# A decode step with paged attention: cache pages requested two page pairs ahead, and the first head of each superblock's attention requested some steps before its first logits

## The chip, the cores and the metric

The kernel runs on one core of a Trainium2 chip. The metric is the device time of one execution in microseconds, from the runs shown, with the median as the kernel's time. One further execution was recorded by the hardware profiler; all rows below come from it.

## The reference, cut to what matters

One layer of a hybrid decoder. A prompt of 2048 tokens (after 16 meta tokens) and 8 samples of 8 new tokens each go through one input projection whose columns are queries, keys, values, and the two inputs of a recurrent branch; then attention and recurrence side by side, an output projection, and a squared-ReLU MLP. The attention is stick-breaking: for each query a running product of "keep" factors goes over the keys from the last to the first.

```python
z = einsum('bqhd,bkhd->bhqk', q, k) * HEAD_DIM ** -0.5 + bias
log_keep = where(mask, log_sigmoid(-z), 0.0)
suffix = cumsum(log_keep, axis=3, reverse=True) - log_keep
w = where(mask, exp(log_sigmoid(z) + suffix), 0.0)
out = einsum('bhqk,bkhd->bqhd', w, v)
```

The samples attend to 512 past positions each, which lie in 4 pages of 128 rows in a key cache and a value cache; a page table says which pages (`cache_k[page_table]`, `cache_v[page_table]`). Everything is float32.

## The kernel before, in words

**The main line.** The prompt is cut into four superblocks of 512 tokens. For each, `inproj` (line 432) multiplies by the input projection: eight `gemm` calls for the recurrent branch (x and gate, alternating), four for keys, one `gemm_nat` of four weight tiles for values, four `gemm` calls for queries. Every float32 matmul is three matmuls of split operands (lines 181 to 183 and 213 to 215): a weight tile `wraw` is loaded on SP, split into `whi` by ACT (line 158) and `wlo` by DVE (line 159). After the four projections come, for each superblock, the output projection (`out_proj`), and the MLP (`up` and `down`, four slices each). The order of TensorE (PE) is written out by hand: it is the order in which the program emits its matmuls. The order on ACT, DVE, POOL and SP is not written by hand; it is set when the program is built, from the dependencies, the buffers that come free and the order of writing, so a load can stand on its queue ahead of instructions that were written before it.

**The side line.** Attention is written as generators that are woven into the main line by the class `Work` (line 37). Each `yield busy, pe` ends a step and states its cost in units; `tick(c)` (line 61), called after every few matmuls of the main line, adds `c * rate` to a debt, and steps are taken until the debt is used up. Three matmuls of 512 columns count 0.64 units of `c`; `gemm` ticks after k = 2, 5 and 7 (line 186, that is `c` of 1.92, 1.92 and 1.28), `gemm_nat` with 1.28 after each row block. The rate is 0.2 during the recurrent part of superblocks 1 to 3, 0.5 in their key, value and query part and in `up`, and 0.55 in `down` (line 1198). The second number of a yield is only added to `work.now`, which nothing reads. The order of the side line is fixed (lines 1101 to 1103): first `sample_attn`, then `attn(0)` to `attn(3)`, each from the time at which its keys and queries are written. `need(key)` (line 74) takes all the steps that are left of a generator at once, without main matmuls between them. `group(0)` (line 1117) calls it for `attn(0)` right after the first query `gemm` of the last superblock (lines 1131 to 1137); two more query `gemm` calls follow (`NQ` is 3), in which `Group.load` fetches the attention's result `md` for the first output projection, and then `out_proj`. The superblocks 1 to 3 are asked for in the same way before the last `down` slice of the superblock ahead.

**The samples' attention** (`sample_attn`, line 809) runs four rounds t_, two samples each. `weights(t_)` makes the logits of the new keys (line 825), then for four page pairs calls `page`, which takes a tile "kv" and issues two indirect DMAs on POOL's queue (line 817), and multiplies (line 840); a chain of sigmoids on ACT, a scan and a product on DVE (`chain`, line 629) makes the weights. `values(t_)` transposes them (lines 855 and 859), copies them to `wt` (tag "q", on ACT) and `wtn` (on DVE, line 861), multiplies the new values (line 869 with `vns`), then again calls `page` for four page pairs and multiplies each (line 869 with `kv`).

**The prompt's attention** (`attn(s)`, line 650) goes over 8 heads; a head has s + 1 groups of keys. `head(h)` (line 658) takes a tile "q" and loads the queries (line 661, 512 KB) and the top keys and values (lines 665 and 666); `kv_load(n)` (line 673) loads the keys and values of one group (lines 678 to 680 or 683 and 684). All go out on POOL's queue. In the generator `s_items` the first step calls `head(0)`, `head(1)`, `kv_load(0)`, `kv_load(1)` and then the first logits (line 694); transposes (line 705, `emit_T`) follow some steps later, are split into `wth` (ACT, line 709) and `wtl` (DVE, line 710), and `emit_V` multiplies (lines 720 and 721). After the last logits of a superblock 13 steps are left: three empty ones, then transposes and value products.

**Buffers.** The tag "kv" has three buffers, shared by the pages and by `kv_load`. The tag "q" has two, shared by `wt` and by the queries of `head`.

Of the kernel before, what the change touches and what calls it, by code (L numbers as in the profile page):

```python
# [84 lines left out]
def _program(tc, I, O, NSB, NSC):  # L85
# [18 lines left out]
    def T(p, shape, dt, tag, bufs=1):  # L104
        uid[0] += 1
        return p.tile(shape, dt, name=f"{tag}_{uid[0]}", tag=tag, bufs=bufs)
# [543 lines left out]
    def attn(s, K):  # L650
# [82 lines left out]
        def s_items():  # L733

            for n, (h, g) in enumerate(groups):
                H = head(h)
                if g == s:
                    head(h + 1) if live["kvt"] < 3 else None
                while live["kv"] > 2:
                    yield None  # L740
                kv_load(n)
                kv_load(n + 1)
                head(h)
                kvt = kvs.pop(n)
                if g == 0:
                    vt = {j: (kvt[:, 400 + P * j:528 + P * j], NMETA + P * j, P) for j in range(3)}
                    vt[-1] = (kvt[0:NMETA, 784:784 + P], 0, NMETA)
                else:
                    vt = {4 * g - 1 + j: (kvt[:, 512 + P * j:640 + P * j], P * j, P) for j in range(4)}
                wtop = None  # L750
                if g == s:
                    while live["w"] >= WB:
                        yield None
                    wtop = logits(H, h, 3, H["kt"][:, 0:P], P, 0)
                    yield 0.6
                ws = []
                for i in range(4):
                    nt = (min(i, 2) + 2) if g == s else 4
                    m = nt * P - (P - NMETA if g == 0 else 0)
                    kap = kvt[:, 0:m]  # L760
                    mask = m - P if (g == s and i < 3) else None
                    while live["w"] >= WB:
                        yield None
                    ws.append(logits(H, h, i, kap, m, mask))
                    if i < 3:
                        yield 1.25 * m / 512
                tl = []
                if g == s:
                    for j in range(3):
                        vap, c0, kn = vt[4 * s + j]  # L770
                        tl.append((vap, kn, j, [(i, ws[i], c0) for i in range(j, 4)]))
                    tl.append((H["kt"][:, P:2 * P], P, 3, [(3, wtop, 0)]))
                    vap, c0, kn = vt[4 * s - 1]
                    tl.append((vap, kn, 0, [(i, ws[i], c0) for i in range(4)]))
                else:
                    for t_ in sorted(vt, reverse=True):
                        vap, c0, kn = vt[t_]
                        tl.append((vap, kn, 0, [(i, ws[i], c0) for i in range(4)]))
                for ti, (vap, kn, i0, parts) in enumerate(tl):
                    e = ti == len(tl) - 1  # L780
                    top = g == s and ti == 3
                    tq.append(dict(at=step[0] + 4, v=vap, kn=kn, i0=i0, parts=parts, H=H, h=h,
                                   first=(g == s and ti == 0), last=(g == 0 and e), endg=e, top=top,
                                   frees=(4 if e else 0) + (1 if top else 0)))
                yield 1.25 * m / 512

        src = s_items()
        more = True
        while more or tq or vq:
# [19 lines left out]
    def sample_attn(K, p1):  # L809
        ck = I["cache_k"]  # L810
        cv = I["cache_v"]

        def page(src, b, pp):
            t = T(att, [P, 2, 512], F32, "kv", 3)
            for e in range(2):
                j = b * NPAGE + 2 * pp + e
                nc.gpsimd.indirect_dma_start(out=t[:, e, :], out_offset=None, in_=src,
                                             in_offset=bass.IndirectOffsetOnAxis(ap=K["ix"][:, j:j + 1], axis=0))
            return t

        def weights(t_):
            sn = psT()
            for c in range(4):
                for bb in range(2):
                    nc.tensor.matmul(sn[32 * c:32 * c + 32, 0:NSAMP], K["Qz"][:, c, t_, bb, :], K["kns"][:, c, :],
                                     start=(bb == 0), stop=(bb == 1))
            zn = T(att, [P, NSAMP], F32, "zn", 1)
            nc.vector.tensor_tensor(zn, sn[:, 0:NSAMP], K["maskS"][:, t_, :], op=ALU.add)
            wn, carry = chain(zn, NSAMP, K["brow"], K["nbrow"], None)
            yield 0.7, 1.0  # L830
            sp = psT()
            nc.tensor.matmul(sp, K["zb"][:, 0:P], K["zb"], start=True, stop=False)
            for bb in range(2):
                for pp in range(2):
                    kp = page(ck, 2 * t_ + bb, pp)
                    yield 0.3, 0.0
                    for e in range(2):
                        g = 2 * pp + e
                        for c in range(4):
                            nc.tensor.matmul(sp[32 * c:32 * c + 32, g * P:(g + 1) * P], K["Qz"][:, c, t_, bb, :],  # L840
                                             kp[:, e, c * P:(c + 1) * P], start=False, stop=False)
                        yield 0.3, 0.3
            nc.tensor.matmul(sp, K["zb"][:, 0:P], K["zb"], start=False, stop=True)
            w, _ = chain(sp, 512, K["brow"], K["nbrow"], carry)
            out[t_] = (w, wn)
            yield 1.8, 0.0

        out = {}
        smix = T(p1, [P, 4, NSAMP], F32, "smix")

        def values(t_):
            w, wn = out[t_]
            tp = psT()
            for pg in range(4):
                nc.tensor.transpose(tp[:, pg * P:(pg + 1) * P], w[:, pg * P:(pg + 1) * P], ident)
            wt = T(att, [P, 4, P], F32, "q", 2)
            nc.scalar.copy(wt.rearrange("p a b -> p (a b)"), tp)
            tp = psT()
            nc.tensor.transpose(tp[0:NSAMP, 0:P], wn[:, 0:NSAMP], ident)
            wtn = T(att, [NSAMP, P], F32, "wtn", 1)  # L860
            nc.vector.tensor_copy(wtn, tp[0:NSAMP, 0:P])
            yield 1.0, 0.6
            yield 1.0, 0.0
            o = psO()

            nc.tensor.matmul(o[:, 0:2 * P], K["zb"][:, 0:P], K["zb"][:, 0:2 * P], start=True, stop=False)

            def av(c, bb, w, v):
                nc.tensor.matmul(o[32 * c:32 * c + 32, bb * P:(bb + 1) * P], w, v, start=False, stop=False)

            for c in range(4):
                for bb in range(2):
                    av(c, bb, wtn[:, 32 * c:32 * c + 32], K["vns"][:, c * P:(c + 1) * P])
            for bb in range(2):
                b = 2 * t_ + bb
                for pp in range(2):
                    vp = page(cv, b, pp)
                    yield 0.3, 0.0
                    for e in range(2):
                        for c in range(4):  # L880
                            av(c, bb, wt[:, 2 * pp + e, 32 * c:32 * c + 32], vp[:, e, c * P:(c + 1) * P])
                        yield 0.3, 0.3
            nc.tensor.matmul(o[:, 0:2 * P], K["zb"][:, 0:P], K["zb"][:, 0:2 * P], start=False, stop=True)
            ot = T(att, [P, 512], F32, "beta", WB)
            nc.scalar.copy(ot[:, 0:2 * P], o[:, 0:2 * P])
            yield 0.5, 0.0
            yield 0.5, 0.0
            tp = psT()
            for bb in range(2):
                nc.tensor.transpose(tp[:, bb * P:(bb + 1) * P], ot[:, bb * P:(bb + 1) * P], ident)  # L890
            ov = tp[:, 0:2 * P].rearrange("p (x c b h q) -> p x c b h q", x=2, c=4, b=2, h=2)
            for hh in range(2):
                r = slice(64 * hh, 64 * hh + 64)
                for bb in range(2):
                    b = 2 * t_ + bb
                    nc.scalar.copy(smix[r, :, b * DS:(b + 1) * DS], ov[r, bb, :, bb, hh, :])
            yield 0.5, 0.2

        for t_ in range(4):
            yield from weights(t_)  # L900
            yield 1.0, 0.0
            yield from values(t_)
        nc.sync.dma_start(msd[:, 0:4, :], smix)
        yield 1.0, 0.0
# [376 lines left out]
```

## Time and profile before

| | us |
|---|---|
| median of 3 runs | 2818.16 (2817.05 to 2828.23) |
| the profiled execution, its own time | 2818.91 |
| its span, first to last instruction | 2817.1 |
| PE busy | 2719.1 (97%) |
| DVE, ACT, POOL busy | 1787.8, 1450.0, 692.4 |
| samples' attention on PE | from 184 to 434 |
| attention of superblock 0 on PE | from 438 to 659 |
| last instruction of superblock 3's attention | 2174 |

The times of rows are microseconds from the start of the span. In a timeline row the first number is the start, the second the duration, then engine, line, operation, what is written from what, and the count of instructions merged into the row; in brackets stands how long the engine was idle before it and what ended that. A matmul's duration reaches past the start of the next one, since matmuls are pipelined. PEclk is the granted TensorE clock as a share of the higher of its two levels, 2.4 GHz; 0.50 is the lower, 1.2 GHz.

### The profile page before, as it was taken

To read this page: it belongs to the slowest core of one execution; us is meant where nothing else is said; L and a number is where in the kernel's file an instruction comes from. 1 tells how busy PE (TensorE), PEld (TensorE's weight loads), DVE (VectorE), ACT (ScalarE), POOL (GpSimd) and SP (SyncE) were. 2 spreads that over 40 slices of the span, in tenths; PEclk is the share of its full clock that TensorE was granted. 3 is DMA by queue.
4 is the path that set the end of the run, shared out by engine and by line. 5 is a ranking of instruction groups with operands and counts; after the bars stand their busy time and mean duration, and the time that the engine had idled before them with its cause. 6 is when DMAs were issued, how large, how long until landed. Compare 5 with 4: busy or idle time off the path is not lost.

```text
span 2817.1 us, 38544 instructions
## 1 busy us (share of the span) xinstructions
PE 2719.1 (97%) x13964; PEld 2219.4 (79%) x13964; DVE 1787.8 (63%) x2412; ACT 1450.0 (51%) x2426; POOL 692.4 (25%) x1351
## 2 busy tenths in 40 slices
PE   8999997998899999999999999999999999999998
PEld 7886756776678888887788888877888887998996
DVE  5445364776776777787867777787676436433434
ACT  5556364675665655566555555665555334332332
POOL 4436371342322221133221221332111002000002
PEclk9999999999899999999999999999999999999999
DMA  4465846567533433345443333454332334322223
GB/s 160 132 205 184 258 142 168 148 176 215 160 99 117 118 112 103 107 137 152 152 109 111 105 106 102 139 160 135 100 103 89 123 120 138 101 80 82 83 83 112
DMA packets 176445, 368.12 MB, mean 131 GB/s; under 512 B 48656, under 2 KB 78480, under 8 KB 176256
## 3 DMA queue, kind: packets, MB, share of 16 engines
q1 hardware_dynamic: 103936, 287.41, 32.2%
q0 software_dynamic: 72320, 78.26, 11.1%
q8 instruction: 110, 1.80, 0.3%
q14 instruction: 79, 0.65, 0.1%
HBM read 305.32 MB, written 60.04 MB: 130 GB/s over the span
## 4 chain that ended last, share of the span: by engine, by line
PE 78%; DVE 7%; DMA 5%; POOL 4%; issue 3%; ACT 2%; SPq 0%; DVEq 0%; another core or an unknown queue 0%; POOLq 0%; ACTq 0%
PE D L181 11%; PE D L213 10%; PE D L214 10%; PE D L182 10%; PE D L215 10%; PE D L183 10%; PE T L694 4%; PE T L705 4%; PE O L720 2%; PE O L721 2%; DMA x1d<-y 1%; DVE pb L643 1%; DMA vd<-vst 1%; DVE wlo L159 1%; POOL rstd L237 1%
## 5 line engine op out<-in xcount | busy, mean ns | idle before, releaser
L159 DVE TENSOR_TENSOR wlo<-wraw,whi 128x1024 fp32r<-128x1024 f32 x368 | 466.4, 1267 | 498.2 <-ACT whi L158 481.7
L181 PE MATMUL D<-ahi,whi 128*128 128x512 f32 (+3 forms) x1920 | 712.1, 371 | 0.7 <-ACT ahi L1002 0.7
L183 PE MATMUL D<-ahi,wlo 128*128 128x512 f32 (+3 forms) x1920 | 686.2, 357 | 3.3 <-DVE wlo L159 3.3
L182 PE MATMUL D<-alo,whi 128*128 128x512 f32 (+3 forms) x1920 | 685.9, 357 | 1.6 <-DVE alo L1003 1.6
L158 ACT CAST whi<-wraw 128x1024 fp32r<-128x1024 f32 x368 | 386.5, 1050 | 481.4 <-PE D L214 283.6
L213 PE MATMUL D<-whi,uh 128*128 128x512 f32 x1024 | 418.5, 409 | 0.0
L183 PEld LDWEIGHTS D<-ahi,wlo 128*128 128x128 f32 x1920 | 364.7, 190 | 54.5 <-DVE wlo L159 4.7
L181 PEld LDWEIGHTS D<-ahi,whi 128*128 128x128 f32 x1920 | 365.0, 190 | 53.3 <-issue 9.5
L214 PE MATMUL D<-whi,ul 128*128 128x512 f32 x1024 | 404.3, 395 | 0.0
L215 PE MATMUL D<-wlo,uh 128*128 128x512 f32 x1024 | 403.9, 394 | 0.0
L182 PEld LDWEIGHTS D<-alo,whi 128*128 128x128 f32 x1920 | 365.8, 191 | 43.5 <-DVE alo L1003 1.8
L634 ACT ACTIVATE keep<-T,nbias 128x512 f32<-128x512 f32 (+6 forms) x352 | 209.5, 595 | 255.3 <-PE T L694 155.5
L643 DVE TENSOR_TENSOR_SCAN pb<-keep,carry 128x512 f32<-128x512 f32 (+1 forms) x228 | 267.8, 1175 | 74.7 <-ACT keep L634 71.2
L710 DVE TENSOR_TENSOR wtl<-T,wth 128x512 fp32r<-128x512 f32 (+4 forms) x352 | 211.9, 608 | 83.7 <-ACT wth L709 82.9
L709 ACT CAST wth<-T 128x512 fp32r<-128x512 f32 (+4 forms) x352 | 183.8, 526 | 125.4 <-PE T L705 121.7
L645 POOL COPY carry<-pb 128x1 f32<-128x1 f32 x360 | 90.3, 251 | 631.8 <-DVE pb L643 624.2
L215 PEld LDWEIGHTS D<-wlo,uh 128*128 128x128 f32 x1024 | 192.3, 188 | 46.6
L646 DVE TENSOR_TENSOR beta<-beta,pb 128x512 f32<-128x512 f32 (+7 forms) x360 | 208.8, 580 | 30.8 <-POOL carry L645 1.0
L213 PEld LDWEIGHTS D<-whi,uh 128*128 128x128 f32 x1024 | 192.7, 188 | 39.0
L214 PEld LDWEIGHTS D<-whi,ul 128*128 128x128 f32 x1024 | 192.9, 188 | 38.3
L635 ACT ACTIVATE beta<-T,bias 128x512 f32<-128x512 f32 (+6 forms) x352 | 208.0, 591 | 0.0
L705 PE MATMUL T<-ident,beta 128*128 128x128 f32 (+1 forms) x1216 | 192.2, 275 | 8.1 <-ACT beta L635 5.6
(233 smaller groups left out, 3836.7 us busy)
## 6 DMA issues: line engine op xcount, KB each, us to landing
wraw<-in_w_up SPq DMA_DIRECT2D x128, 512.0 KB
wraw<-in_w_down SPq DMA_DIRECT2D x128, 512.0 KB
wraw<-in_w_in SPq DMA_DIRECT2D x64, 512.0 KB
q<-qd POOLq DMA_DIRECT2D x32, 512.0 KB, 17.3
wraw<-in_w_out SPq DMA_DIRECT2D x32, 512.0 KB
kv<-kd POOLq DMA_DIRECT2D x48, 256.0 KB, 3.6
kv<-vd POOLq DMA_DIRECT2D x48, 256.0 KB, 5.9
y<-in_x_prompt SPq DMA_DIRECT2D x16, 512.0 KB
```

Of the source, the lines that this page charges most:

```text
L158: nc.scalar.copy(hi, r)
L159: nc.vector.tensor_tensor(lo, r, hi.bitcast(F32), op=ALU.subtract)
L181: nc.tensor.matmul(o, whi[:, k, :], ahi(k, a, b), start=(k == 0), stop=False)
L182: nc.tensor.matmul(o, whi[:, k, :], alo(k, a, b), start=False, stop=False)
L183: nc.tensor.matmul(o, wlo[:, k, :], ahi(k, a, b), start=False, stop=(k == KC - 1))
L213: nc.tensor.matmul(o, h, whi[:, kk, :], start=st, stop=False)
L214: nc.tensor.matmul(o, l, whi[:, kk, :], start=False, stop=False)
L215: nc.tensor.matmul(o, h, wlo[:, kk, :], start=False, stop=sp)
L634: nc.scalar.activation(keep[:, 0:n], S, AF.Sigmoid, bias=nbias, scale=-0.125)
L643: nc.vector.tensor_tensor_scan(pb[:, 0:n][:, ::-1], kr, kr, init, op0=ALU.mult, op1=ALU.bypass)
L705: nc.tensor.transpose(t[0:kn, i * P:(i + 1) * P], w[:, c0:c0 + kn], ident)
L710: nc.vector.tensor_tensor(lo[0:kn, cs], t[0:kn, cs], hi[0:kn, cs].bitcast(F32), op=ALU.subtract)
```

## The change

`sample_attn` gets a list of all 32 page pairs in the order in which they are used. The old `page` becomes `fetch`; the new `page` first fetches until three pairs are in hand and returns the oldest, so a pair's DMAs are written two pairs before its first use. Two pairs are fetched before the first round. The number of buffers stays three. Between `weights` and `values` of each round there is one more empty step of 1.0 unit, and the second number of one yield goes from 1.0 to 0.5. `attn(s)` calls `head(0)` and `kv_load(0)` at once and then takes four empty steps of 0.6 units before the first step of `s_items`, which then calls `head(1)`, `kv_load(1)` and makes the first logits.

```diff
@@ -784,6 +784,10 @@ attn
+        head(0)
+        kv_load(0)
+        for _ in range(4):
+            yield 0.6, 0.0
         src = s_items()
@@ -810,7 +814,17 @@ sample_attn
-        def page(src, b, pp):
+        pages = [(src, 2 * t_ + bb, pp) for t_ in range(4) for src in (ck, cv) for bb in range(2) for pp in range(2)]
+        ready, at = [], [0]
+
+        def page():
+
+            while len(ready) < 3 and at[0] < len(pages):
+                ready.append(fetch(*pages[at[0]]))
+                at[0] += 1
+            return ready.pop(0)
+
+        def fetch(src, b, pp):
             t = T(att, [P, 2, 512], F32, "kv", 3)
@@ -827,12 +841,12 @@ weights
-            yield 0.7, 1.0
+            yield 0.7, 0.5
...
-                    kp = page(ck, 2 * t_ + bb, pp)
+                    kp = page()
@@ -845,6 +859,9 @@
+        ready.append(fetch(*pages[0]))
+        ready.append(fetch(*pages[1]))
+        at[0] = 2
@@ -874,7 +891,7 @@ values
-                    vp = page(cv, b, pp)
+                    vp = page()
@@ -898,6 +915,7 @@
             yield from weights(t_)
+            yield 1.0, 0.0
             yield 1.0, 0.0
             yield from values(t_)
```

## Rows read from the trace of the kernel before

**Rows 1.** The page: busy time of the engines, and the chain's shares.
```profile
PE 2719.1 (97%) x13964; PEld 2219.4 (79%) x13964; DVE 1787.8 (63%) x2412; ACT 1450.0 (51%) x2426; POOL 692.4 (25%) x1351
...
PE 78%; DVE 7%; DMA 5%; POOL 4%; issue 3%; ACT 2%; SPq 0%; DVEq 0%; another core or an unknown queue 0%; POOLq 0%; ACTq 0%
```

**Rows 2.** PE's groups by form: count, busy and mean, idle before and its releaser.
```profile
L869 PE MATMUL O<-kv,q 128*32 128x128 f32 x256 | 12.5, 299 | 10.3 <-DMA kv<-in_cache_v,ix 10.3
L694 PE MATMUL T<-kvt,q 128*128 128x128 f32 x64 | 12.0, 271 | 6.2 <-DMA q<-qd 6.2
```

**Rows 3.** Stretches of PE: length, busy, PEclk, DMA share, GB/s.
```profile
400.00:470.00 70.00, 53.92 (x283) 0.85 0.56 155
...
428.00:432.00 4.00, 4.00 (x23) 0.50 0.12 36
...
454.60:459.60 5.00, 4.93 (x17) 0.52 0.66 205
```

**Rows 4.** Timeline, POOL: the fourth key page, after the first one's last matmul.
```profile
192.33 1.12 POOL L817 DMA_INDIRECT kv<-in_cache_k,ix  x1 [2.44 <-PE T L840]
```

**Rows 5.** Timeline, PE and POOL: value pages of round 0, first to fourth.
```profile
242.68 0.64 PE L869 MATMUL O<-kv,q 128*32 128x128 f32 x16
...
242.81 2.05 POOL L525 TENSOR_TENSOR gt<-g 128x512 f32<-128x512 f32 x1 [0.67 <-ACT g L522]
...
248.31 1.01 POOL L817 DMA_INDIRECT kv<-in_cache_v,ix  x1
...
251.71 0.43 PE L869 MATMUL O<-kv,q 128*32 128x128 f32 x8 [1.44 <-DMA kv<-in_cache_v,ix]
...
253.93 0.42 PE L869 MATMUL O<-kv,q 128*32 128x128 f32 x8 [1.80 <-DMA kv<-in_cache_v,ix]
```

**Rows 6.** Timeline, POOL and PE: the fourth value page of round 1.
```profile
288.73 0.98 POOL L817 DMA_INDIRECT kv<-in_cache_v,ix  x1 [9.79 <-PE O L869]
...
295.98 0.43 PE L869 MATMUL O<-kv,q 128*32 128x128 f32 x8
```

**Rows 7.** Timeline, PE, POOL and DVE: round 3 from its transposes to the fourth value page.
```profile
401.86 0.60 PE L855 MATMUL T<-ident,beta 128*128 128x128 f32 x4
...
409.11 1.10 PE L869 MATMUL O<-vns,wtn 64*32 64x128 f32 x16 [2.85 <-DVE wtn L861]
...
409.35 0.91 POOL L661 DMA_DIRECT2D q<-qd  x1
...
416.21 1.31 POOL L817 DMA_INDIRECT kv<-in_cache_v,ix  x1 [0.16 <-issue]
...
427.77 0.50 POOL L680 DMA_DIRECT2D kv<-vmd  x1 [5.47 <-DMA q<-qd]
...
427.89 0.65 PE L869 MATMUL O<-kv,q 128*32 128x128 f32 x8 [7.03 <-DMA kv<-in_cache_v,ix]
```

**Rows 8.** Timeline, POOL and PE: the second head of superblock 0.
```profile
434.25 0.83 POOL L661 DMA_DIRECT2D q<-qd  x1 [5.98 <-issue]
...
454.67 0.66 PE L694 MATMUL T<-kvt,q 128*128 128x128 f32 x2 [6.21 <-DMA q<-qd]
```

**Rows 9.** Timeline, POOL and PE: the first head of superblock 1.
```profile
617.61 0.81 POOL L661 DMA_DIRECT2D q<-qd  x1 [0.41 <-issue]
...
662.27 0.52 PE L694 MATMUL T<-kvt,q 128*128 128x128 f32 x2
```

**Rows 10.** Timeline, PE: the last value product of superblock 0.
```profile
658.26 0.50 PE L720 MATMUL O<-wth,kv 16*128 16x512 f32 x1 [2.74 <-ACT wth L709]
```

**Rows 11.** Timeline, PE: a transpose that waited for its own chain.
```profile
492.87 0.33 PE L705 MATMUL T<-ident,beta 128*128 128x128 f32 x1 [3.88 <-ACT beta L635]
```

**Rows 12.** Timeline, PE: start of the first output projection; ACT: its load.
```profile
682.43 0.50 PE L215 MATMUL D<-wlo,ahi 128*128 128x512 f32 x1 [1.47 <-DVE wlo L159]
...
689.59 0.50 PE L213 MATMUL D<-whi,ahi 128*128 128x512 f32 x1 [2.36 <-DVE sl L603]
...
676.55 1.05 ACT L937 CAST ahi<-x 128x1024 fp32r<-128x1024 f32 x1 [6.18 <-DMA x<-md]
```

## The prediction

> **What bounds the kernel now.** I read the page first: PE is busy 97% of the span, with 78% of the chain that ended last on it [rows 1]. So a change that takes no matmul away can only win what PE idles, 98 us in all (2817.1 minus 2719.1), and what it loses at the lower clock. The second view, PE's groups, says which of that belongs to this change: 10.3 us before the value pages' matmuls, all released by the page's DMA, and 6.2 us before a head's first logits, released by the query load [rows 2]. The third view, stretches of PE, shows that both lie together: between 400 and 470 PE is busy 53.9 of 70 us, so 16.1 idle, at a mean granted clock of 0.85 [rows 3]. The rest of PE's idle time belongs to norms and weight splits, which the change doesn't touch. This is the ceiling: 16.5 us of waits (10.3 and 6.2) and some 4 us of clock.
>
> **Are the pages late because they are asked for late?** The timeline of POOL says mostly not. The fourth key page goes out right behind the matmul that frees its buffer [rows 4]; the build has already moved the request up, and three buffers, not the place in the text, hold it back. So does round 1's fourth value page: PE released POOL after 9.79 us, and PE used the page 7.3 us after the request (295.98 minus 288.73) without waiting [rows 6]. In round 0 POOL was late: PE's matmuls with the first page were over at 243.3 (242.68 plus 0.64), POOL was in gate products from 242.81, the request went out at 248.31, and PE waited 1.44 and 1.80 [rows 5]. In round 3 the request at 416.21 stands behind the 512 KB query load of superblock 0's first head, issued at 409.35 on the same queue; that load lands at 427.77, the page's matmul starts at 427.89 after 7.03 us [rows 7].
>
> **The change, part by part.**
> *Pages written two pairs earlier.* No DMA is added, and the buffers stay three. What can change is the order on POOL. In round 0 the page may go ahead of the gate products: up to 3.2 us won (1.44 plus 1.80). Against it, rounds 1 and 2, which don't wait now, may catch what round 0 has, up to 3.2 us each. I take a gain of 2.0, since the waiting round also comes later (below) while the gate products don't.
> *The extra step in each round.* One unit four times, so the samples' attention ends 4.0 units later, and by its place in the key and value part (rate 0.5) that is 8 units of main work, which the planner counts as microseconds. It is covered by gemms, and no matmul is added: cost nothing by itself. It moves round 3 past the gate products and scans that made `wtn` 2.85 us late [rows 7]; rounds 0 to 2 don't wait there. But a round that gets there 2.85 us earlier meets the same query load: from transposes to the fourth page PE would need 16.2 us (427.89 minus 7.03 minus 2.85 minus 401.86), the load went out 7.5 us after the transposes and took 18.4. If POOL sends it 3 to 7 us after them, the page lands 21 to 26 us after them, and PE waits 5 to 10 us where it now waits 9.9 in sum (7.03 plus 2.85). I take 2.5 won; the bounds are 9.9 won plus 2 of clock (4 us at 0.50 [rows 3]), and 3 lost.
> *Four steps before the first logits.* The first heads are not late now: superblock 1's queries go out 45 us before their use [rows 9], and superblock 0's first at 409.35 [rows 7], with the first logits at 438. So `head(0)` and `kv_load(0)` (three loads of queries, keys and values, two or three of a group, all on POOL's queue, no more than now) gain nothing. What the four steps do is to hold back what follows: 2.4 units, at rate 0.5 some 4.8 us of main work. The wait that exists is the second head's: its "q" buffer comes free only with round 3's last value matmul, its load goes out at 434.25, lands 20.4 us later, and PE waits 6.21 [rows 8]. `head(1)` still goes out when the buffer is free, its logits come 4.8 us later: about 1.5 us of wait are left, so 4.7 won. The 5 us at 0.52 behind that wait [rows 3] cost about 2.4; I take 2.0 won. Bounds: 8.6 won in all; nothing, if `head(1)`, now written behind the four steps, also goes out 4.8 us later.
> *What is late next: the end of superblock 0's attention.* Now its last value product starts at 658.26 and the next attention at 662.27 [rows 10, 9], in the ticks after k = 2 and k = 5 of the first query gemm of superblock 3. `need` comes after that gemm, so between the end and `need` lie two ticks, 0.96 and 0.64 units at rate 0.5: 1.6 units to spare. The change uses 6.4 (4.0 and 2.4). Then 4.8 units are left undone, and the 13 steps after the last logits cost 4.65 by the planner's numbers (three empty ones 0.9; transposes 0.6, 0.45, 0.3, 0.3, 0.6 with value products beside them; one more 0.3 between; four steps with products at 0.3). So the whole tail of head 7 is taken at once, without gemms between. PE then waits for its chain: 3.88 as where a transpose waited for its chain before [rows 11], less about 1.3 for the six matmuls still between, then for a cast, 2.74 as in [rows 10], and half of that again at the last product. That is 6.7, less the 2.74 that this tail waits now: 4.0 lost (bounds 0 and 10).
> *And behind that.* After the drain the debt is some 4.8 below zero, so the next superblock's logits come some ten ticks later, in the output projection. The two query gemms and the start of the projection then run without casts and scans of logits on ACT and DVE; there PE now waits 1.47 and 2.36 [rows 12]. I take 2.0 won of the 3.8; up to 5 could be lost if head 7's result, now written about 10 us later, holds back `Group.load`: ACT already stands 6.18 us for such a load [rows 12]. The later superblocks' shifts (2.4 units each) cost nothing: their attention ends at 2174, with over 600 us of gemms behind it.
>
> Sum: 2.0 + 2.5 + 4.7 + 2.0 - 4.0 + 2.0 = 9.2 us won. The profiled execution took 2818.91 (the span of 2817.1 and 1.8 around it), 0.75 above the median; so 2809.7 for it, and 2809.0 against the median, which is my forecast.
>
> **The rivals.** *All waits go* (the page goes ahead of the query load, the drain is hidden): 3.2 + 9.9 + 2 + 8.6 + 3.8 = 27.5 won, 2791. For it speaks that all of these waits stand within 60 us of each other; against it the one queue that carries 512 KB ahead of the page. *Nothing moves:* the requests went out when the buffers came free, and still do; the waits only change places, and what the second head wins the drain takes back: 2818. For it speak [rows 4, 6]. The Trainium skill has a rule that speaks for it too: "Perfetto Trace Analysis", section "Identifying Performance Opportunities", says that a gap that repeats on the engine that should be saturated can mean too few buffers for the next tile, and this change adds none. By that rule the pages' 2.0 in my sum would be zero and the total 2811; round 1, without a wait on the same three buffers, speaks against it here. *Slower:* the drain holds the output projection. Place: `need` after the first query gemm. If the undone steps exceed the tail (they do by 0.2), head 7's result reaches `Group.load` too late, and SP's queue, which has the output projection's weights behind that load, stands too. Price: the drain at its bound, 10, and ACT's and SP's stand of 6.2 once more with 5 at the projection, 21 in all; 2818 + 21 - 6.7 for the second head = 2832, and 2839 if that gain is lost as well. It decides once head 7's result is in place later than 26 us after that gemm (two query gemms and the projection's first weight tile at 5.1 by the planner, and 11 for the drain with its matmuls); I work out 24 (the drain's 11, some 6 for the result's write and 6.2 for its load, taken alike, and the cast's 1.05 [rows 12]).
>
> **How the numbers follow.** About 0.5% (14 us) is what a measurement of this kernel can tell from no change. The forecast's own case has 0.55, all waits go 0.2, nothing moves 0.17, slower 0.08. The ends of the terms hardly come together; their distances from what I took, added as squares, make 10.6 us to the fast side (1.2, 9.4, 1.9, 4.0, 1.8) and 15.2 to the slow (8.4, 5.5, 6.7, 6.0, 7.0), so 2798 to 2824, and hold two of the cases. The range is 2795 to 2826, which leaves out most of the first rival and of the last. Faster by over 0.5%, below 2804: the first rival and a fifth of the forecast's own case (0.11), 0.31. Slower, above 2832: 0.06. Within: 0.63.
>
> **What would show it.** The profile of the changed kernel should show the second head's wait on the query load at under 2 us where it is 6.21; the wait before round 3's last page still there, at 4 to 9 us with its half-clock stretch, right when the first query load lands; the fourth page of each round still requested at the earliest by the first page's last matmul; `head(0)` of superblocks 1 to 3 issued as far ahead as now; and a stretch near 665 with transposes and value products without gemms between, and waits on ACT and DVE in it. The forecast is wrong if the pages of round 3 pass the query load, if head 7's tail is still woven into gemms, or if the output projection starts with a wait of over 5 us.

## The result, and the profile after

| | before | after |
|---|---|---|
| median of 6 runs each, side by side | 2818.91 us (2817.05 to 2828.23) | 2833.07 us (2830.74 to 2840.48) |
| ratio, 95% interval | | 1.0052 [1.004, 1.0065] |
| profiled execution | 2818.91, span 2817.1 | 2832.24, span 2830.5 |

The changed kernel is slower by some 14 us. The forecast was 2809, faster by 9, with a range up to 2826: the sign was wrong and the range didn't hold the time. The time is that of the rival "slower" (2832 to 2839), and the largest single loss stands at that rival's place (10.6 us, by stages below); but a run that takes its drain away, further down, doesn't get the time back.

The page of the changed kernel, engines and chain, against [rows 1]:

```profile
PE 2719.0 (96%) x13964; PEld 2217.7 (78%) x13964; DVE 1787.2 (63%) x2412; ACT 1450.3 (51%) x2426; POOL 690.6 (24%) x1351
...
PE 80%; DVE 6%; DMA 5%; POOL 4%; ACT 3%; issue 3%; SPq 0%; DVEq 0%; POOLq 0%; ACTq 0%
```

No engine does more than before: PE has the same 13964 matmuls and 2719 us. PE's idle time went from 98.0 to 111.5 us (span less busy), which is the difference of the spans (its busy time is equal only in sum: the first stretch of the views below has 8.7 us less of it, the others together as much more, in part at a lower clock). PE's groups by form say which waits these are (columns as in [rows 2]):

```profile
L886 PE MATMUL O<-kv,q 128*32 128x128 f32 x256 | 12.8, 291 | 10.4 <-DMA kv<-in_cache_v,ix 10.4
L694 PE MATMUL T<-kvt,q 128*128 128x128 f32 x64 | 11.6, 263 | 0.0
L720 PE MATMUL O<-wth,kv 128*128 128x384 f32 x32 | 13.1, 410 | 7.5 <-ACT wth L709 7.5
L721 PE MATMUL O<-wtl,kv 128*128 128x512 f32 x224 | 89.2, 398 | 6.6 <-DVE wtl L710 6.6
L213 PE MATMUL D<-whi,ahi 128*128 128x512 f32 x384 | 158.5, 413 | 6.7 <-DVE sl L603 6.5 <-ACT whi L158 0.3
```

The two waits that the change aims at stand first. The value pages' is what it was, 10.4 for 10.3 (L869 is now L886); the query load's is gone, 0.0 for 6.2. Below them are waits that the kernel before had small or not at all, on ACT and DVE: in its groups L720 with 384 columns stands with 0.0, L721 with 0.9, L213 with 3.2.

**By stages.** The next two views are stretches of PE (length, busy, PEclk, DMA share, GB/s), first of the kernel before, then of the changed one; each edge is at the same matmul of the main line in both, within a microsecond.

```profile
0.00:60.00 60.00, 49.21 (x245) 1.00 0.53 174
...
400.00:495.00 95.00, 74.76 (x385) 0.88 0.59 166
...
640.00:740.00 100.00, 92.41 (x436) 0.98 0.65 189
740.00:801.00 61.00, 48.24 (x229) 0.83 0.48 143
...
1300.00:1400.00 100.00, 93.55 (x455) 1.00 0.55 172
...
1850.00:1950.00 100.00, 95.41 (x458) 0.98 0.56 170
```

```profile
0.00:52.40 52.40, 40.51 (x246) 1.00 0.61 200
...
396.00:480.00 84.00, 67.08 (x350) 0.90 0.59 175
...
626.00:734.00 108.00, 95.58 (x432) 0.92 0.61 177
734.00:797.00 63.00, 46.54 (x229) 0.86 0.50 142
...
1296.00:1400.00 104.00, 94.92 (x463) 0.97 0.58 170
...
1848.00:1954.00 106.00, 99.11 (x470) 0.95 0.51 165
```

What a stretch loses is its length less busy time times PEclk: idle time and lower clock together. The samples' last round and the first heads (400 to 495) lose 29.2 us before and 23.6 after: 5.6 won, where the forecast saw its gains. The end of superblock 0's attention with the output projection loses 9.4 and 20.1: 10.6 lost, 4.8 of it idle and 5.8 at a lower clock. Behind it come 2.0 lost in the norms of superblock 0, 5.5 in those around 1300 and 5.4 around 1850. The stretches left out add 2.3 of idle time. Together 20.2 lost; 7.6 of that comes back in the first row, the start, 60.0 long in one profile and 52.4 in the other, which has nothing to do with the change (last section). So 12.6, beside 13.4 between the spans; the views round PEclk to 0.01, and the rest is not resolved.

The places, in the timeline of PE in the changed kernel (rows as in [rows 5]):

```profile
248.29 0.43 PE L886 MATMUL O<-kv,q 128*32 128x128 f32 x8 [2.71 <-DMA kv<-in_cache_v,ix]
...
315.31 0.43 PE L854 MATMUL T<-kv,Qz 128*32 128x128 f32 x8 [2.55 <-DMA kv<-in_cache_k,ix]
...
429.60 0.66 PE L886 MATMUL O<-kv,q 128*32 128x128 f32 x8 [7.32 <-DMA kv<-in_cache_v,ix]
...
456.35 0.33 PE L694 MATMUL T<-kvt,q 128*128 128x128 f32 x2
...
476.80 0.69 PE L720 MATMUL O<-wth,kv 128*128 128x384 f32 x1 [7.52 <-ACT wth L709]
...
652.39 0.49 PE L721 MATMUL O<-wtl,kv 16*128 16x512 f32 x1 [1.50 <-DVE wtl L710]
...
654.77 0.59 PE L720 MATMUL O<-wth,kv 128*128 128x512 f32 x1 [0.75 <-ACT wth L709]
...
683.27 0.79 PE L213 MATMUL D<-whi,ahi 128*128 128x512 f32 x1 [6.49 <-DVE sl L603]
...
760.71 0.79 PE L721 MATMUL O<-wtl,kv 128*128 128x512 f32 x1 [6.64 <-DVE wtl L710]
...
1324.20 0.47 PE L261 MATMUL T<-ident,y 128*128 128x128 f32 x1 [6.00 <-DVE y L1007]
```

Rows 476.80, 683.27, 760.71 and 1324.20 are four waits of 6 to 7.5 us on casts, splits and norms. Two of them are followed up in ACT's timeline:

```profile
470.39 0.59 ACT L562 COPY sf<-D 128x512 f32<-128x512 f32 x1 [6.27 <-DMA out_v_prompt<-sf]
...
475.06 0.59 ACT L565 CAST vst<-D 128x512 fp32r<-128x512 f32 x1 [3.14 <-DMA vd<-vst]
...
476.26 0.48 ACT L709 CAST wth<-T 128x384 fp32r<-128x384 f32 x1
...
676.96 1.04 ACT L955 CAST ahi<-x 128x1024 fp32r<-128x1024 f32 x1 [5.06 <-DMA x<-md]
...
681.07 0.58 ACT L602 CAST sh<-D 128x512 fp32r<-128x512 f32 x1
```

At 476.80 PE wants `wth`, which is made at 476.26. In ACT's order, ahead of it stand the copy and the cast of two value blocks of the input projection, which wait for the stores of earlier blocks (6.27 and 3.14). The store that the cast waits for was issued at 462.40, while the 512 KB query load of the third head was in flight (issued at 457.46, landing 16.6 us later); the next store but one was issued at 477.30 with no query load in flight. From issue to landing they took, in this order:

```profile
DMA to landing us min/median/max: 12.6/12.6/12.6
...
DMA to landing us min/median/max: 5.4/5.4/5.4
```

At 683.27 PE waits for `sl`, which needs the cast `sh` of 681.07; that stands behind the load of head 7's result `md` (5.06).

### The profile page after: what moved, and what is told of

The parts are those of the page before. It is cut to its first block, busy times and chain, and to the rows that moved or that the text cites. A ratio compares the mean times of both kernels' runs of the same rounds, so it can differ in the third digit from the quotient of the medians.

```text
span 2830.5 us, 38536 instructions
## 1 busy us (share of the span) xinstructions
PE 2719.0 (96%) x13964; PEld 2217.7 (78%) x13964; DVE 1787.2 (63%) x2412; ACT 1450.3 (51%) x2426; POOL 690.6 (24%) x1351
## 4 chain that ended last, share of the span: by engine, by line
PE 80%; DVE 6%; DMA 5%; POOL 4%; ACT 3%; issue 3%; SPq 0%; DVEq 0%; POOLq 0%; ACTq 0%
PE D L181 11%; PE D L183 11%; PE D L182 11%; PE D L213 10%; PE D L214 10%; PE D L215 10%; PE T L705 4%; PE T L694 4%; PE O L720 2%; PE O L721 2%; DVE pb L643 1%; DVE wlo L159 1%; DMA x1d<-y 1%; POOL rstd L237 1%; DMA md<-keep 1%
## 5 line engine op out<-in xcount | busy, mean ns | idle before, releaser
L182 PE MATMUL D<-alo,whi 128*128 128x512 f32 (+3 forms) x1920 | 685.2, 357 | 1.6 <-DVE alo L1021 1.6
L213 PE MATMUL D<-whi,uh 128*128 128x512 f32 x1024 | 418.7, 409 | 0.4 <-DVE uf L1036 0.4
L183 PEld LDWEIGHTS D<-ahi,wlo 128*128 128x128 f32 x1920 | 363.7, 189 | 52.4 <-DVE wlo L159 2.2
L182 PEld LDWEIGHTS D<-alo,whi 128*128 128x128 f32 x1920 | 364.8, 190 | 43.8 <-DVE alo L1021 1.8
L645 POOL COPY carry<-pb 128x1 f32<-128x1 f32 x360 | 83.0, 231 | 649.9 <-DVE pb L643 647.1
L213 PEld LDWEIGHTS D<-whi,uh 128*128 128x128 f32 x1024 | 193.4, 189 | 41.4 <-issue 1.1
## 6 DMA issues: line engine op xcount, KB each, us to landing
q<-qd POOLq DMA_DIRECT2D x32, 512.0 KB, 16.6
```

The costliest lines, as they stand in the source:

```text
L182: nc.tensor.matmul(o, whi[:, k, :], alo(k, a, b), start=False, stop=False)
L183: nc.tensor.matmul(o, wlo[:, k, :], ahi(k, a, b), start=False, stop=(k == KC - 1))
L213: nc.tensor.matmul(o, h, whi[:, kk, :], start=st, stop=False)
```

## The experiments

Each was timed in five rounds beside the kernel before on the same chip; its ratio is against those runs. None leaves out any of the computation.

**First question: which part of the change is slow?** The theory was the empty steps (1.0 unit in each of four rounds, 2.4 at the head of each superblock's attention), which push superblock 0's attention into `need`, so that its tail is drained there. The rival was the new order of the pages on POOL's queue.

*Pages alone:* the changed kernel without any of its empty steps and without `head(0)`, `kv_load(0)` ahead.

```diff
-        head(0)
-        kv_load(0)
-        for _ in range(4):
-            yield 0.6, 0.0
...
-            yield 1.0, 0.0
```

> Only the page pairs written two ahead; no added steps, no head requested early. Theory A (the loss comes from the added steps, 6.4 units until superblock 0's attention ends): the planner's order of PE is unchanged, so within 3 us of before, 2816 to 2822, attention of superblock 0 ending before need as in before, and the second head's wait on its query load still about 6. Theory B (the pages' requests, written earlier, change the order on POOL for the worse): most of the 14 us lost is here, 2828 to 2833, with a key page's wait in round 2 as in the changed kernel (3 us).

Measured: 2823.22 beside 2821.87, ratio 1.0011 [1.0002, 1.002].

*The round's step alone:* the kernel before with the second `yield 1.0, 0.0` between `weights` and `values`.

```diff
             yield from weights(t_)
+            yield 1.0, 0.0
             yield 1.0, 0.0
```

> Only the empty step of 1.0 unit in each round of the samples' attention (4.0 units). Theory A: the attention of superblock 0 ends 2.4 units short of done at need, so part of its tail is drained; the second head's wait stays at about 6; loss 4 to 10 us, 2823 to 2829. Theory B: no change, 2816 to 2822.

Measured: 2839.44 beside 2821.87, ratio 1.0069 [1.0056, 1.0082].

*Four steps alone*, in every `attn(s)`, with nothing loaded ahead:

```diff
+        for _ in range(4):
+            yield 0.6, 0.0
         src = s_items()
```

> Only the four empty steps of 0.6 at the start of each superblock's attention; nothing is requested earlier. Theory A: the second head's wait falls from 6.2 to under 2, 0.8 units are left at need (2.4 less 1.6), so hardly anything is drained; 5 to 8 us won, 2810 to 2814, if the later superblocks' shifts cost nothing; near 2819 if they do. Theory B: 2810 to 2814 as well, so this run tells what the shifts cost, not what the pages do.

Measured: 2840.83 beside 2821.87, ratio 1.0069 [1.0054, 1.0085].

*Heads alone:* `head(0)` and `kv_load(0)` written ahead, no step.

```diff
+        head(0)
+        kv_load(0)
         src = s_items()
```

> Only head(0) and kv_load(0) written ahead, with no step between. Theory A: the loads already went out when their buffers came free, so nothing moves: 2816 to 2821, and superblock 1's first query load goes out over 40 us ahead of its use as before. Rival: the order of head(1) and kv_load(0) on POOL's queue changes the second head's wait by more than 2 us either way.

Measured: 2822.43 beside 2821.87, ratio 1.0002 [0.9992, 1.0011].

The two parts that request data earlier do next to nothing; either set of empty steps alone costs 18 to 19 us, more than the whole change. So the parts don't add, and a sum of separate prices can't be right. Both theories missed these two runs: the first had 4 to 10 us lost for the round's step, the second nothing, and for the four steps neither had a loss. With the round's step alone PE also waits 4.65 and 5.62 for casts at the start of the output projection, so the drain may have a part in that run. In the timeline of PE with the four steps alone the second head's wait is gone, and larger ones stand near the places where the kernel before had 3.88 [rows 11] and 2.74 [rows 10]; the last two rows are ACT's, which stands just ahead of each for the store of a value block:

```profile
489.03 0.90 PE L705 MATMUL T<-ident,beta 128*128 128x128 f32 x3 [9.43 <-ACT beta L635]
...
667.93 0.76 PE L720 MATMUL O<-wth,kv 128*128 128x512 f32 x1 [9.38 <-ACT wth L709]
...
486.65 0.58 ACT L565 CAST vst<-D 128x512 fp32r<-128x512 f32 x1 [7.98 <-DMA vd<-vst]
...
664.71 0.58 ACT L565 CAST vst<-D 128x512 fp32r<-128x512 f32 x1 [8.11 <-DMA vd<-vst]
```

**Second question: is it the drain?** From here on the theories are "drain" (the steps cost because head 7's tail is taken at once in `need`) and "alignment" (they cost because each later attention step now meets another place of the main line, and other work ahead of it in the order of ACT, DVE and POOL).

*No drain:* the changed kernel with a higher rate in the key, value and query part of superblock 3, so that superblock 0's attention ends before `need`.

```diff
-        work.rate = RATE1 if s else 0.0
+        work.rate = (RATE1 + 0.12 if s == NSB - 1 else RATE1) if s else 0.0
```

> The changed kernel with the planner's rate in the last superblock's key, value and query part at 0.62 in place of 0.5, some 5 units more, so that superblock 0's attention is done before need again. Theory drain (the tail taken at once at need, and the projection's load behind it, cost most of the 14 us): 2818 to 2824, and the waits of 2 to 7 us between 640 and 690 gone. Theory alignment (each shift of the side line against the main line meets other casts and loads on the in-order queues of ACT, DVE and POOL, and the kernel before stood well): these waits go but others come in the same stretch or in those behind it, 2826 to 2836.

Measured: 2834.67 beside 2820.31, ratio 1.0051 [1.0039, 1.0063], as the changed kernel itself. So the loss doesn't need the drain. What the drain costs by itself this run can't tell, since the higher rate is a shift too. The timeline of PE shows the start of the projection mended (1.63 for 6.49), and new waits elsewhere:

```profile
479.18 0.69 PE L720 MATMUL O<-wth,kv 128*128 128x384 f32 x1 [8.60 <-ACT wth L709]
...
663.53 0.58 PE L720 MATMUL O<-wth,kv 128*128 128x256 f32 x1 [6.61 <-ACT wth L709]
...
692.67 0.50 PE L213 MATMUL D<-whi,ahi 128*128 128x512 f32 x1 [1.63 <-DVE sl L603]
```

*Two or four steps in superblock 0 alone*, in the kernel before. Two steps are 1.2 units, less than the 1.6 that the prediction found to spare, so nothing is drained.

```diff
+        for _ in range(2 if s == 0 else 0):
+            yield 0.6, 0.0
         src = s_items()
```

> The kernel before with two empty steps of 0.6 at the start of superblock 0's attention alone: 1.2 units, less than the 1.6 to spare at need, so nothing is drained. Theory drain: the second head's wait falls by some 2.4 and nothing else, 2817 to 2819 against 2820 of before. Theory alignment: new waits for casts and scans of 3 us and more between 460 and 790, and a time that can lie 5 to 15 above before.

Measured: 2826.31 beside 2818.65, ratio 1.0029 [1.0019, 1.0039]. With `range(4 if s == 0 else 0)`:

> Four steps, 2.4 units, at the start of superblock 0's attention alone. Theory drain: the second head's wait is gone and 0.8 units are drained, 2813 to 2817. Theory alignment: the stretch from 440 to 800 is as in the run with four steps in all superblocks, and the time lies 8 to 19 above before, the part that is not owed to the later superblocks.

Measured: 2833.05 beside 2818.65, ratio 1.0063 [1.0047, 1.0078]. Without a drain 1.2 units already cost 7.7 us; in that kernel's profile superblock 0's last value products indeed stand ahead of the last six matmuls of the first query `gemm`, so before `need`. (The profiled execution took 2820.98, the fastest of its eleven, so its rows show less than the median's loss.) Its largest new wait in the timeline of PE is again near [rows 11] with its 3.88, and again behind a store that ACT waits for:

```profile
481.24 0.69 PE L705 MATMUL T<-ident,beta 128*128 128x128 f32 x2 [8.61 <-ACT beta L635]
...
479.38 0.58 ACT L565 CAST vst<-D 128x512 fp32r<-128x512 f32 x1 [6.28 <-DMA vd<-vst]
```

*The steps in superblocks 1 to 3 alone.* The prediction had put these at nothing, since over 600 us of gemms follow.

```diff
+        for _ in range(4 if s else 0):
+            yield 0.6, 0.0
         src = s_items()
```

> Four steps at the start of superblocks 1 to 3 only; all up to the end of superblock 0's attention is as before. The prediction's term: nothing, 2818 to 2822, as over 600 us of gemms lie behind the last attention. Theory alignment: new waits behind 660, in the bursts before the first MLP (740 to 800) and around 1320 and 1880, 3 to 12 above before.

Measured: 2836.13 beside 2818.65, ratio 1.0065 [1.005, 1.0081]: 17 us, from a delay with over 600 us of gemms behind it. That is more than either theory had. One of its waits can be followed further. In PE's timeline the last transpose of `y` in superblock 0's MLP waits 6.30, where the kernel before waits 1.61:

```profile
1325.36 0.48 PE L261 MATMUL T<-ident,y 128*128 128x128 f32 x1 [6.30 <-DVE y L991]
```

DVE's timeline in this kernel, then in the kernel before (L986 and L984 are the residual addition of a row block, L991 and L989 its norm):

```profile
1306.55 1.28 DVE L986 SCALAR_TENSOR_TENSOR y<-y,rstd,x 128x1024 f32<-128x1024 f32 x1 [1.11 <-POOL rstd L237]
...
1313.84 0.76 DVE L991 TENSOR_SCALAR y<-y,rstd 128x1024 f32<-128x1024 f32 x1 [2.96 <-DMA x1d<-y]
...
1317.93 0.75 DVE L991 TENSOR_SCALAR y<-y,rstd 128x1024 f32<-128x1024 f32 x1 [2.06 <-DMA x1d<-y]
1318.60 1.28 DVE L986 SCALAR_TENSOR_TENSOR y<-y,rstd,x 128x1024 f32<-128x1024 f32 x1
...
1324.56 0.74 DVE L991 TENSOR_SCALAR y<-y,rstd 128x1024 f32<-128x1024 f32 x1
```

```profile
1314.96 1.28 DVE L984 SCALAR_TENSOR_TENSOR y<-y,rstd,x 128x1024 f32<-128x1024 f32 x1 [0.51 <-POOL rstd L237]
1316.16 0.75 DVE L989 TENSOR_SCALAR y<-y,rstd 128x1024 f32<-128x1024 f32 x1
...
1322.26 0.75 DVE L989 TENSOR_SCALAR y<-y,rstd 128x1024 f32<-128x1024 f32 x1 [1.21 <-DMA x1d<-y]
```

Before, the fourth block's addition (1314.96) stands ahead of the third block's norm (1316.16). With the steps it stands behind it (1318.60 behind 1317.93), and that norm waits for the store of its block. So the fourth block's addition starts 3.64 us later, though the main line was at the matmul of 1300 some 3.5 us earlier than before (1296.5, after a quicker start). The order is one part of it, the stores are another. The second block's store, issued at 1304.35, lands 9.5 us later, and the third block's norm follows its addition by over 11 us (1306.55 to 1317.93) where it took 6 before (1310.05 to 1316.16). A head's query load was in flight here, issued at 1295.12 and landing 24.3 us later; in the kernel before none goes out between 1286.13 and 1345.

In the changed kernel the order is swapped too (the third block's norm at 1310.96), but that costs nothing there: the fourth block's addition comes at 1311.78, ahead of the 1314.96 of before. Its norm then waits 6.88 for the block's store; the query load of a head went out just ahead of that store (DVE's and POOL's timelines):

```profile
1311.78 1.29 DVE L1002 SCALAR_TENSOR_TENSOR y<-y,rstd,x 128x1024 f32<-128x1024 f32 x1
...
1323.40 0.75 DVE L1007 TENSOR_SCALAR y<-y,rstd 128x1024 f32<-128x1024 f32 x1 [6.88 <-DMA x1d<-y]
...
1311.69 0.84 POOL L661 DMA_DIRECT2D q<-qd  x1
```

So the wait of 6.00 at 1324.20 is a late store's. The delayed attention did not use up DVE; it changed the order in which the build put DVE's instructions, and it moved a query load to where the main line waits for its stores.

*Earlier in place of later:* the kernel before without the step that it has between `weights` and `values`.

```diff
             yield from weights(t_)
-            yield 1.0, 0.0
```

> The opposite shift: the empty step of 1.0 that each round of the samples' attention has before is taken out, so all that follows comes up to 4.0 units earlier. Theory drain: more to spare at need, 2816 to 2820. Theory alignment (the kernel before stands in a good place, and a shift to either side costs): 2824 to 2838, with other waits for casts and scans in the stretch from 440 to 800.

Measured: 2820.75 beside 2818.65, ratio 1.0012 [1.0001, 1.0023]. A shift to the other side costs 2 us, not 5 or more: a miss for alignment put as "any other place is worse"; the number of theory drain, 2816 to 2820, is nearer. The waits do move there too (round 3's page wait is gone, the second head's is 7.81 for 6.21); here wins and losses nearly cancel.

**Third question: can the waits be taken away?**

*The value blocks' copies.* In the changed kernel ACT stands 6.27 us for the store of `sf` (row 470.39). Here two of the four blocks take other buffers.

```diff
-            vf = stage("sf", F32)[:, 0:512]
+            vf = (stage("sf", F32) if t in (0, 1) else T(p1, [P, W], F32, "g") if t < 4 and t % 2 == 0 else T(p1, [P, W], F32, "xc", 1))[:, 0:512]
```

> The changed kernel, with the float copies of the value blocks 2 and 3 in two other buffers, so that ACT no longer waits for the store of an earlier block. If that store is what ACT stood on (6.27 us before the cast that PE waited 7.52 for): that wait goes or falls under 3, 5 to 8 us won, 2825 to 2828. If ACT then waits for the next store on its way (that of the split values, 3.14 in the same stretch), under 4 won.

Measured: 2832.91 beside 2820.31, ratio 1.0046 [1.0033, 1.0059]. The wait on `sf` is gone and ACT stands on the next store instead; PE waits 6.97 where it waited 7.52. ACT's timeline:

```profile
471.04 0.59 ACT L565 CAST vst<-D 128x512 fp32r<-128x512 f32 x1 [9.38 <-DMA vd<-vst]
```

*The query buffers.* `wt` takes one of the three buffers of "wth", so that "q" has both of its own for queries; first in the kernel before, then in the changed one.

```diff
-            wt = T(att, [P, 4, P], F32, "q", 2)
+            wt = T(att, [P, 4, P], F32, "wth", 3)
```

> The kernel before with the samples' transposed weights in the tag wth in place of q, so that both query buffers are free for superblock 0's first two heads from the start. Expected if the query buffer is what makes round 3's last page and the second head late: both query loads go out before 300, the waits of 7.03 and 6.21 and the half-clock behind them go, 15 to 18 us won, 2803 to 2807. Rival (the queue, not the buffer): the loads go out early but the page still waits over 4 us: 2812 or more.

Measured, in the kernel before: **2803.31** beside 2820.31, ratio 0.9937 [0.9924, 0.9949], 17 us faster than the kernel before, and so ahead of both.

> The changed kernel with the same tag for the transposed weights. If the change's loss is the shift alone, the page's wait of 7.32 goes here too and the rest of the loss stays: 8 to 10 us won against the changed kernel, 2822 to 2826, and some 18 us above the kernel before with this tag.

Measured, in the changed kernel: 2830.85 beside 2820.31, ratio 1.0034 [1.0021, 1.0047]; about 2 us won of the 8 to 10 expected, a miss.

In the faster one the timeline of POOL shows the first two query loads 245 and 269 us ahead of where they were [rows 7, 8]:

```profile
163.88 0.82 POOL L661 DMA_DIRECT2D q<-qd  x1 [5.04 <-DMA qd<-sl]
165.28 0.84 POOL L661 DMA_DIRECT2D q<-qd  x1
```

They go out as soon as the queries are written (released by that DMA). So no query load stands ahead of round 3's pages: their wait is 0.33 where it was 7.03, and the second head doesn't wait. To ask early, the build lacked only a buffer. The Trainium skill, "Perfetto Trace Analysis", section "Identifying Performance Opportunities", says that a repeating gap on the engine that should be saturated can mean too few buffers for the next tile; this run agrees, with 17 us for one buffer freed in "q" (no buffer was added in all). In the changed kernel the page's wait shrinks too, from 7.32 to 3.69, and the one for `wth` near 472 from 7.52 to 4.72; the other new waits remain.

## Why the prediction was wrong

**The failed step.** "The extra step in each round ... cost nothing by itself" and "the later superblocks' shifts cost nothing". Both were priced by what the steps contain (nothing) and by what ends last behind them (gemms). The runs show 17.6 us (four rounds' steps), 14.4 (four steps in superblock 0) and 17.5 (superblocks 1 to 3), each alone. A step without work delays every later piece of attention against PE's fixed order, and the build then orders ACT, DVE and POOL differently. It also set aside the idle time of "norms and weight splits, which the change doesn't touch"; around 1300 and 1850, at the norms of later superblocks, the stages lost 5.5 and 5.4. The prediction looked at waits that exist and asked which shrink; it didn't ask which cover that now holds with little to spare would be lost. Four waits of over 6 us came up at places for which it had no term, or one with the wrong sign. Where a wait was followed to a store of the main line, for which ACT or DVE stood, a query load of the delayed attention was in flight beside that store, and such stores land late (last section).

Term by term, from the two profiles:

| term | forecast | measured |
|---|---|---|
| round 0's pages [rows 5] | 2.0 won | 3.24 to 2.71: 0.5 won; new in round 2: 0.58 and 2.55 lost |
| round 3, `wtn` and page [rows 7] | 2.5 won | `wtn` 2.85 to 0, page 7.03 to 7.32: 2.6 won, but 1.44 new before its transposes |
| second head [rows 8] | 4.7 won | 6.21 to 0: 6.2 won |
| superblock 0's tail | 4.0 lost | waits of 2.46 (1.50, 0.75, 0.21) for 2.96 (2.74, 0.22): nothing lost |
| start of the output projection [rows 12] | 2.0 won | 3.83 to 7.39 (0.26, 0.64, 6.49): 3.6 lost, and a lower clock behind |
| all other delays | 0 | 476.80, 760.71, 1324.20 and more |

**What was right.** The first heads gain nothing, and the pages hardly what it gave them (2.0), since buffers and not the place in the text hold them back: 1.0002 and 1.0011 alone. Round 3's page still waits for the query load that stands ahead of it on POOL's queue, issued at 409.20, with the page's requests from 417.46 on. The second head's wait went. The tail of head 7 was indeed taken at once, from 649.9 to 659.2 without a gemm.

**The rival "slower"** had its place right (ACT standing for `md`, 5.06, and the projection late by 6.49), but "no drain" removes that and the time stays; that its number came out is in part luck. Its chance of 0.08 was too small for another reason: every mechanism that the prediction could price was at a known wait.

**What stays open.** Why a given shift costs what it does: 1.2 units 7.7 us, 2.4 units 14.4, one unit less in each round 2.1, and 6.4 units with both parts about 14. One case (around 1318) was followed to a swapped order on DVE and late stores, one (1324.20) to a late store alone, three (476.80, and 489.03 and 481.24 in other kernels) to stores ahead of ACT's work; 760.71 was only located. That the query load is what makes the stores late is seen in the profiles, not tested by a run that moves that load alone.

## What to carry to other kernels

Where one engine's order is fixed by hand and the others' is built around it, an empty step need not be free: it moves all later side work against that order, and its price is set by covers with little to spare, not by existing waits (here 8 to 19 us for added steps, and 2 for one taken out). See where the side work's big loads would come to lie, and whether the main line waits for stores there. Before moving a request earlier, see in the trace whether it already goes out when its buffer comes free; if so, look for a buffer: here one was worth 17 us where earlier text was worth nothing. Time each part of such a change alone and together, since the parts don't add.

## What the runs showed of the hardware

**Stores beside a large load.** The main line's 512 KB stores go out on SP, the 512 KB query loads on POOL. In the fourteen profiles together, between 400 and 2000 us and as far as landings are recorded, the store of a residual block (`x1d<-y`) landed 2.6 to 6.5 us after its issue in 67 cases with no query load in flight when it was issued, and 6.5 to 10.8 us in 18 of 20 cases with one (5.1 and 5.5 in the other two). The store of a value block (`vd<-vst`) took 3.3 to 8.4 us in 25 cases without, and 8.7 to 16.3 us in 26 with. Other transfers differ between these cases too, so this is what stands together, not a tested cause.

**The start.** The start of the program differs from one profile to the next. The first stretch of the two stage views holds the same work (245 and 246 records), but PE is busy 49.21 us with it in the profile of before and 40.51 in that of after, with PEclk recorded as 1.00 in both; the main line was at the same matmul 7.8 us earlier (60.12 and 52.36). In the twelve experiments' profiles it got there between 52.3 and 55.8, kernels before and changed alike, so the profile of before is the odd one. In it the matmuls of L182 with 272 columns take 428 ns each between 15 and 30 us, and 287 between 42 and 50: PE ran slower at first, whatever PEclk says there. No kernel was profiled twice, so how often one kernel starts this way is not known. A comparison of two single profiles can be off by 8 us from this, over half of what was to be explained here; the ratios stand on the timed runs.
